# RWKV recurrences of a two-block kernel: the batches of a chunked recurrence reordered, and their triangular inverse started from blocks of 16 instead of 32

## The chip, the cores and the metric

The kernel runs on one core of a Trainium2 chip as one program. The metric is the device time of one execution in microseconds (us). Five engines work side by side, each through a list of instructions in a fixed order: PE (TensorE, matrix products), DVE (VectorE), ACT (ScalarE), POOL (GpSimd) and SP, which here only issues DMA transfers. They wait for each other through semaphores.

## What is computed

Two blocks follow each other on 512 tokens of width 1024. The first holds a Hyena branch and an RWKV-7 branch, whose gated sum goes through an output projection, and then a mixture of 16 experts. The second holds sparse attention, two feed-forward layers and an S5 layer. The change lies in the RWKV branch, and the gates that stand beside it come from the same projection:

```python
def rwkv_scan(decay, k, v, a_vec, b_vec, r, state0, reverse):
    def step(S, inp):
        w_t, k_t, v_t, a_t, b_t = inp[:5]
        sa = jnp.einsum('bhij,bhj->bhi', S, a_t)
        S = S * w_t[:, :, None, :] + sa[..., None] * b_t[:, :, None, :] + v_t[..., None] * k_t[:, :, None, :]
        y = jnp.einsum('bhij,bhj->bhi', S, inp[5]) if emit else None
        return S, y
...
def token_mixer(h, p, states0):
    cols = h @ p['w_in']
    hy_cols, rw_cols, gate_cols = jnp.split(cols, (HY_COLS, HY_COLS + RW_COLS), axis=-1)
    y_hy = hyena_branch(hy_cols, p) @ p['hy_proj']
    y_rw, finals = rwkv_branch(rw_cols, p, states0)
    g_hy, g_rw = jnp.split(jax.nn.sigmoid(gate_cols), 2, axis=-1)
    mixed = (g_hy * y_hy + g_rw * (y_rw @ p['rw_proj'])) @ p['w_out']
```

The recurrence runs over 8 heads of 64, in both directions, over 512 tokens, after a run over 256 context tokens that leaves the first states.

## The kernel before

The recurrence is cut into chunks of 64 tokens. Within a chunk the effect of the removal vectors on each other is a unit lower triangular 64x64 system; its inverse turns the chunk into a map of the state, and only those maps are applied one after the other. The work is done in six batches (`rwkv`, L627): two of the context tokens (256 columns, no read-out) and four of the latent tokens (512 columns, one group of two heads and both directions each). A batch holds 16 chunk systems and goes through these steps:

- `rw_start` (L749): projections of the hidden state (`win_mm`, PE at L614 for the context and, split in three fp32r products, at L285 to L287 for the latent tokens), neighbour mixing on DVE (L621, L622), norms through `head_rstd` (PE L726, DVE, a power on POOL at L733, PE L735 and L741), decays (PE L800, a scan on DVE L805), and the scaled vectors AR and BK.
- `rw_gram` (L845): the products of these vectors within a chunk (PE L866), masked into the tile GA (DVE L875). GA has one buffer.
- `rw_inverse` (L887): a transposition into 32x32 blocks (DVE L894), then 31 steps of substitution on DVE, each one product (L902) and one sum (L903) on 31 to 256 elements per partition.
- `rw_blocks` (L906): two transpositions (DVE L913 into X, L914 into TTt), then the lower left 32x32 block of each 64x64 inverse from 32 small products (PE L923), a copy (ACT L926), and 32 more (PE L931).
- `rw_rows` and `rw_ops` (L936, L1006): transpositions and products that build the chunk maps (PE L956 to L1023, L1036), the sum into MT (DVE L1027) and the start of SP (L1039).
- `rw_chain` (L1047): for the latent batches seven steps in each of two directions, in each a PE product (L1066) and a DVE sum (L1071), then the read-out on PE (L1084, L1087).
- `rw_end` (L701): the normalisation of the read-out (PE L707, `head_rstd` again on the tile rny, DVE L712).

The small products L923 and L931 use 32x32 quadrants of the PE array (`tile_position`), many others 64x64 quarters or all of it.

Two more pieces of PE work stand in this stage. `hy_out` (L543) projects the Hyena output. `fill` (L548) computes the gates: 16 groups of columns, each 24 fp32r products (384 in all) into the one PSUM buffer "sm", an activation on ACT into the tile hyo (one buffer), a scaling on POOL and a transfer to memory:

```python
        for w_, dst in (("wgh", self.mhd), ("wgr", self.grd)):
            for c in range(KD):
                ps = self.psum("sm", 1)
                self.h_mm(ps, I[w_][c], "wf", self.nwf, nc.gpsimd)
                g = self.rw["wk"].tile([P, T], F32, name="hyo")
                nc.scalar.activation(g, ps, AF.Tanh, scale=0.5)
```

`fill` is written last, but the program is put in order by a scheduler when it is built: it sets one order of instructions for each engine, after dependences, its own estimates and the order of writing, and puts products of `fill` and of the next batch between others. Buffers are handed out by tags with a number of buffers each; a new tile waits for the last reader of the tile whose buffer it takes. After the stage `mix_out` reads the gates back (tile mhg), projects the recurrence's output (PE L1295, L1303, tiles rwp), multiplies by the gates and goes into the output projection (PE L285 to L287 with woh, wol).

Of the kernel before, what the change touches and what calls it, by code (L numbers as in the profile page):

```python
# [12 lines left out]
F32 = mybir.dt.float32  # L13
# [4 lines left out]
AF = mybir.ActivationFunctionType  # L18
OP = mybir.AluOpType
# [47 lines left out]
def _consts():  # L67
# [31 lines left out]
    misc["gmask"] = np.where(i[None, :] < 64, s[:, None] < q, s[:, None] <= q) * 1.0  # L99
    misc["inv"] = np.repeat((10000.0 ** (-np.arange(32, dtype=f8) / 32))[None, :], P, 0)  # L100
    misc["eye16"] = (i[:, None] % 16 == np.arange(16)[None, :]) * 1.0
    misc["iota"] = np.repeat(np.arange(T)[None, :], P, 0) * 1.0
# [76 lines left out]
class K:  # L179
# [444 lines left out]
    mtag = "ch"  # L624
    nmm, nwi, nwf, wit = 2, None, 6, "w"

    def rwkv(self):  # L627
# [4 lines left out]
        es = ExitStack()  # L632
        self.nwi, self.wit = 5, "wi"
        with es:
# [26 lines left out]
            self.rw_gram(B[0])  # L661
            for i in range(len(B) + 1):
                if i < len(B):
                    self.rw_inverse(B[i])
                if i:
                    self.rw_chain(B[i - 1])
                if i and B[i - 1]["out"]:
                    self.rw_end(B[i - 1])
                if i < len(B):
                    self.rw_blocks(B[i])  # L670
                    self.rw_rows(B[i])
                if i + 1 < len(B):
                    self.rw_start(B[i + 1])
                    self.rw_gram(B[i + 1])
                if i == 0:
                    self.hy_out()
                    self.rw_gate()
# [71 lines left out]
    def rw_start(self, b):  # L749
# [23 lines left out]
        if out:  # L773
            b["kms"] = wk.tile([P, T], F32, name="kms", bufs=3)
            b["y"] = wk.tile([P, T], F32, name="yr")
# [69 lines left out]
    def rw_gram(self, b):  # L845
# [3 lines left out]
        nc, out = self.nc, b["out"]  # L849
        g = b["GA"] = self.rw["wk"].tile([P, 2, 2, 8, CH], F32, name="GA", bufs=1)  # L850
        gs = [g]
# [35 lines left out]
    def rw_inverse(self, b):  # L887
        nc, page = self.nc, self.rw_page
        V, G = nc.vector, nc.gpsimd
        GA = b["GA"]  # L890


        L = page("L", "i0").rearrange("p (t s) -> p t s", s=32)
        V.transpose(L, ap(GA, 0, [[1, 32], [32, 2], [CH, 16]]))  # L894
        Xi = page("Xi", "i1").rearrange("p (t s) -> p t s", s=32)
        G.memset(Xi, 0.0)
        G.memset(ap(Xi, 0, [[33, 32]]), 1.0)
        tmp = page("Xt", "i2", 256)
        for s in range(31):
            m, k = 31 - s, s + 1  # L900
            o = tmp[:, :m * k].rearrange("p (t s) -> p t s", s=k)
            V.tensor_tensor(o, L[:, s + 1:, s:s + 1].to_broadcast([P, m, k]), Xi[:, s:s + 1, :k].to_broadcast([P, m, k]), op=OP.mult)  # L902
            V.tensor_tensor(Xi[:, s + 1:, :k], Xi[:, s + 1:, :k], o, op=OP.add)  # L903
        b["Xi"] = Xi

    def rw_blocks(self, b):  # L906
# [3 lines left out]

        TTt = b["TTt"] = wk.tile([P, 16, 64], F32, name="TTt", bufs=1)
        X1 = page("X1", "i0").rearrange("p (u s) -> p u s", s=32)
# [4 lines left out]

        FT = page("FT", "i1", T).rearrange("p (u t) -> p u t", t=32)
        pf = self.psum("ch", 2)
# [16 lines left out]
    def rw_rows(self, b):  # L936
# [13 lines left out]
        for z, gg in enumerate(groups):  # L950
# [13 lines left out]

            AG = self.rw_page("AG", f"i{z}").rearrange("p (n h x c) -> p n h x c", n=4, h=2, x=2)
            ps = self.psum("ch", 2)
# [39 lines left out]
    def rw_ops(self, b, TA):  # L1006
# [4 lines left out]
        BKt, UV, PC, out = (b[x] for x in ("BKt", "UV", "PC", "out"))  # L1011
        MT = b["MT"] = C["wk"].tile([P, 2, 8, CH], F32, name="MT", bufs=1)
        SP = b["SP"] = C["wk"].tile([P, 16, CH], F32, name="SP", bufs=1)
# [1426 lines left out]
```

## Time and profile before

| | |
|---|---|
| median of three runs | 3376.53 us (3373.27 to 3382.11) |
| the profiled execution | 3368.45 us, span of its instructions 3366.7 us |
| PE busy | 3116.9 us, 93% |
| DVE busy | 1637.9 us, 49% |
| ACT, POOL busy | 941.6 us (28%), 733.7 us (22%) |
| mean granted PE clock | 0.95 of full speed |
| the six batches and the end of `fill` | 308 to 922 us of the span |

Busy time is the time in which an engine has an instruction under way; a wait for a semaphore isn't counted. The granted clock is the speed that the chip gave PE, as a share of its full clock. The profiled execution is 8.1 us shorter than the median of the runs, so times worked out from its rows are of its scale. The stage of the change is a fifth of the span.

### The profile page before, as it was taken

To read this page: it belongs to the slowest core of one execution; us is meant where nothing else is said; L and a number is where in the kernel's file an instruction comes from. 1 tells how busy PE (TensorE), PEld (TensorE's weight loads), DVE (VectorE), ACT (ScalarE), POOL (GpSimd) and SP (SyncE) were. 2 spreads that over 40 slices of the span, in tenths; PEclk is the share of its full clock that TensorE was granted. 3 is DMA by queue.
4 is the path that set the end of the run, shared out by engine and by line. 5 is a ranking of instruction groups with operands and counts; after the bars stand their busy time and mean duration, and the time that the engine had idled before them with its cause. 6 is when DMAs were issued, how large, how long until landed. Compare 5 with 4: busy or idle time off the path is not lost.

```text
span 3366.7 us, 42701 instructions
## 1 busy us (share of the span) xinstructions
PE 3116.9 (93%) x16973; PEld 1971.9 (59%) x16973; DVE 1637.9 (49%) x2862; ACT 941.6 (28%) x1707; POOL 733.7 (22%) x793
## 2 busy tenths in 40 slices
PE   8988989889899999999999988899898998999999
PEld 3746666656574334333333256566677777778887
DVE  3665566765361210110110156875676776456464
ACT  3313444323231111111101032245331332234242
POOL 1022233443120233330000033200695002110000
PEclk9999888888889999999999999889998998999999
DMA  5643111111469999999999954310336456322221
GB/s 218 231 168 119 57 41 58 51 35 43 150 245 382 369 421 421 421 421 421 420 421 420 421 220 152 123 57 26 116 124 232 156 194 173 122 88 91 97 100 69
DMA packets 144591, 681.41 MB, mean 202 GB/s; under 512 B 25455, under 2 KB 33815, under 8 KB 76424
## 3 DMA queue, kind: packets, MB, share of 16 engines
q1 hardware_dynamic: 134480, 652.44, 50.6%
q0 software_dynamic: 5536, 18.16, 1.5%
q10 hardware_dynamic: 4376, 8.09, 0.7%
q8 instruction: 134, 2.20, 0.3%
q14 instruction: 65, 0.53, 0.0%
HBM read 654.50 MB, written 24.12 MB: 202 GB/s over the span
## 4 chain that ended last, share of the span: by engine, by line
PE 45%; DMA 15%; DVE 7%; POOL 7%; issue 2%; ACT 2%; SPq 0%; POOLq 0%; ACTq 0%; DVEq 0%
DMA we<-in_w_dram 13%; PE mm L1638 9%; PE mm L285 4%; PE mm L286 4%; PE mm L287 4%; PE ch L1670 3%; POOL cug L2054 3%; PE tr L1552 2%; POOL sca L2055 2%; PE sm L286 1%; PE sm L287 1%; PE sm L285 1%; DMA wa<-in_adaw_dram 1%; PE sm L1601 1%; POOL qss L1896 1%
## 5 line engine op out<-in xcount | busy, mean ns | idle before, releaser
L1638 PE MATMUL mm<-we,XG 128*64 128x512 f32 x2048 | 473.6, 601 | 4.0 <-DMA we<-in_w_dram 3.2
L285 PE MATMUL mm<-hh,wh 128*128 128x512 f32 x704 | 282.6, 402 | 21.4 <-DVE vg L2008 17.0
L1638 PEld LDWEIGHTS mm<-we,XG 128*64 128x64 f32 x2048 | 134.0, 137 | 273.3 <-issue 254.3
L286 PE MATMUL mm<-hl,wh 128*128 128x512 f32 x704 | 278.3, 395 | 0.0
L1670 PE MATMUL ch<-we,hid 128*64 128x512 f32 x1024 | 263.1, 598 | 12.9 <-DMA we<-in_w_dram 12.8
L287 PE MATMUL mm<-hh,wl 128*128 128x512 f32 x704 | 272.9, 396 | 0.0
L1593 DVE SCALAR_TENSOR_TENSOR hth<-hth,tr 128x256 f32<-128x256 f32 x64 | 26.9, 421 | 394.9 <-ACT hth L1592 394.4
L1670 PEld LDWEIGHTS ch<-we,hid 128*64 128x64 f32 x1024 | 94.4, 136 | 170.5 <-issue 133.9
L285 PEld LDWEIGHTS mm<-hh,wh 128*128 128x128 f32 x704 | 134.4, 191 | 63.9 <-issue 27.6
L347 DVE SCALAR_TENSOR_TENSOR macc<-wa,cvs,macc 128x512 f32<-128x512 f32 (+1 forms) x119 | 152.6, 1298 | 20.1 <-DMA wa<-in_adaw_dram 18.2
L470 POOL TENSOR_TENSOR X<-X,gy 128x512 f32<-128x512 f32 x20 | 28.2, 1432 | 590.6 <-DVE gy L1740 590.6
L280 DVE TENSOR_TENSOR wl<-wu,wh 128x1024 fp32r<-128x1024 f32 x88 | 115.2, 1310 | 76.4 <-ACT wh L279 76.2
L287 PEld LDWEIGHTS mm<-hh,wl 128*128 128x128 f32 x704 | 134.7, 191 | 29.7
L286 PEld LDWEIGHTS mm<-hl,wh 128*128 128x128 f32 x704 | 135.2, 192 | 26.9 <-POOL hl L464 0.3
L1606 DVE TENSOR_TENSOR acc<-acc,sm 128x512 f32<-128x512 f32 x48 | 32.9, 686 | 236.4 <-PE sm L1601 236.4
L1649 ACT ACTIVATE hs<-mm 128x512 f32<-128x512 f32 x64 | 38.2, 597 | 387.0 <-PE mm L1638 387.0
L279 ACT ACTIVATE wh<-wu 128x1024 fp32r<-128x1024 f32 x88 | 93.3, 1060 | 130.6 <-PE mm L286 97.6
L287 PE MATMUL mm<-hTh,wl 128*128 128x512 f32 x208 | 89.6, 431 | 13.9 <-DVE wl L280 13.8
L280 DVE TENSOR_TENSOR wl<-wd,wh 128x1024 fp32r<-128x1024 f32 (+1 forms) x48 | 56.0, 1168 | 95.3 <-ACT wh L279 90.9
L1723 POOL TENSOR_TENSOR ess<-ess,mhalf 128x1 f32<-128x1 f32 x4 | 3.2, 791 | 442.8 <-DVE ess L1722 442.7
L279 ACT ACTIVATE wh<-wd 128x1024 fp32r<-128x1024 f32 (+1 forms) x48 | 47.5, 989 | 164.0 <-PE sm L287 75.0
L285 PE MATMUL mm<-hTh,wh 128*128 128x512 f32 x208 | 89.7, 431 | 2.6 <-ACT wh L279 1.9
(835 smaller groups left out, 6685.4 us busy)
## 6 DMA issues: line engine op xcount, KB each, us to landing
we<-in_w_dram SPq DMA_DIRECT2D x384, 1024.0 KB, 14.7
wu<-in_wupf_dram SPq DMA_DIRECT2D x44, 1024.0 KB, 4.8
wa<-in_adaw_dram SPq DMA_DIRECT2D x24, 1024.0 KB, 5.1
wa<-in_adaw_dram SPq DMA_DIRECT2D x96, 256.0 KB, 4.5
wa<-in_modw_dram SPq DMA_DIRECT2D x16, 1024.0 KB, 6.1
wd<-in_wdn_dram SPq DMA_DIRECT2D x16, 1024.0 KB, 4.7
aw<-in_awin_dram SPq DMA_DIRECT2D x12, 1024.0 KB, 5.6
wi<-in_win_dram SPq DMA_DIRECT2D x46, 256.0 KB, 2.7
```

The costliest lines, as they stand in the source:

```text
L279: self.nc.scalar.activation(h, x, AF.Copy)
L280: (E or self.nc.vector).tensor_tensor(l, x, h.bitcast(F32), op=OP.subtract)
L285: mm(ps, a[0], b[0], start=start, stop=False)
L286: mm(ps, a[0], b[1], start=False, stop=False)
L287: mm(ps, a[1], b[0], start=False, stop=stop)
L347: V.scalar_tensor_tensor(a, w, c, a, op0=OP.mult, op1=OP.add)
L1552: nc.tensor.matmul(ps[:, c * i:c * i + c], self.xn[:, t, o:o + P], oh[:, t], start=(t == 0), stop=(t == TT - 1), skip_group_check=True)
L1638: mm = nc.tensor.matmul(ps[64 * h:64 * h + 64], XG[:, k, CAP * e:CAP * e + CAP], w[:, i, h], start=(k == 0), stop=(k == KD - 1), skip_grou ...
L1649: nc.scalar.activation(hs, ps, AF.Copy)
L1670: mm = nc.tensor.matmul(py[n][64 * h:64 * h + 64], hid[h][:, f], ww[h][:, i, 512 * n:512 * n + 512], start=(f == 0), stop=(f == 15), skip_ ...
L2054: E.tensor_tensor(u[k], p[k][1], p[k][0], op=OP.mult)
L2055: E.tensor_tensor(o, u[0], u[1], op=op)
```

## The change

Six things change together. The loop over the batches is written in another order: the start and the Gram products of batch i+1 come before the inverse, blocks, rows, chain and end of batch i, where before the inverse of a batch came first, then the chain of the batch before it. GA gets two buffers. The substitution runs on the 16x16 diagonal blocks alone, both of a 32x32 block in one instruction: 15 steps of two instructions. `rw_blocks` puts the 32x32 inverses together from them: 64 products of 32x32 (after: L924), a copy on ACT, 64 products of 16 columns (L931, L934), 32 more (L939) and four masked sums on DVE (L944, L946, two of L949), ahead of the two sets of 32 products that put the 64x64 inverses together as before. Buffers are moved: wf (weights of `fill`) 6 to 4, wi 5 to 4, kms 3 to 2; TTt and MT share one buffer, FT, F and AG another. What is computed is the same.

```diff
@@ -98,6 +98,7 @@
+    misc["rm"] = np.stack([i % 64 < 16, i % 64 // 16 == 2, i % 64 // 16 == 1], 1) * 1.0
@@ -622,7 +623,7 @@
-    nmm, nwi, nwf, wit = 2, None, 6, "w"
+    nmm, nwi, nwf, wit = 2, None, 4, "w"
@@ -630,7 +631,7 @@
-        self.nwi, self.wit = 5, "wi"
+        self.nwi, self.wit = 4, "wi"
@@ -659,19 +660,16 @@
             self.rw_start(B[0])
             self.rw_gram(B[0])
-            for i in range(len(B) + 1):
-                if i < len(B):
-                    self.rw_inverse(B[i])
-                if i:
-                    self.rw_chain(B[i - 1])
-                if i and B[i - 1]["out"]:
-                    self.rw_end(B[i - 1])
-                if i < len(B):
-                    self.rw_blocks(B[i])
-                    self.rw_rows(B[i])
+            for i, b in enumerate(B):
                 if i + 1 < len(B):
                     self.rw_start(B[i + 1])
                     self.rw_gram(B[i + 1])
+                self.rw_inverse(b)
+                self.rw_blocks(b)
+                self.rw_rows(b)
+                self.rw_chain(b)
+                if b["out"]:
+                    self.rw_end(b)
@@ -771,7 +769,7 @@
-            b["kms"] = wk.tile([P, T], F32, name="kms", bufs=3)
+            b["kms"] = wk.tile([P, T], F32, name="kms", bufs=2)
@@ -847,7 +845,7 @@
-        g = b["GA"] = self.rw["wk"].tile([P, 2, 2, 8, CH], F32, name="GA", bufs=1)
+        g = b["GA"] = self.rw["wk"].tile([P, 2, 2, 8, CH], F32, name="GA", bufs=2)
@@ -896,11 +894,13 @@
-        for s in range(31):
-            m, k = 31 - s, s + 1
-            o = tmp[:, :m * k].rearrange("p (t s) -> p t s", s=k)
-            V.tensor_tensor(o, L[:, s + 1:, s:s + 1].to_broadcast([P, m, k]), Xi[:, s:s + 1, :k].to_broadcast([P, m, k]), op=OP.mult)
-            V.tensor_tensor(Xi[:, s + 1:, :k], Xi[:, s + 1:, :k], o, op=OP.add)
+        for s in range(15):
+            m, k = 15 - s, s + 1
+            o = tmp[:, :2 * m * k].rearrange("p (x t s) -> p x t s", x=2, s=k)
+            at = 32 * (s + 1)
+            V.tensor_tensor(o, ap(L, at + s, [[528, 2], [32, m], [0, k]]), ap(Xi, at - 32, [[528, 2], [0, m], [1, k]]), op=OP.mult)
+            x = ap(Xi, at, [[528, 2], [32, m], [1, k]])
+            V.tensor_tensor(x, x, o, op=OP.add)
         b["Xi"] = Xi
@@ -908,14 +908,48 @@
-        TTt = b["TTt"] = wk.tile([P, 16, 64], F32, name="TTt", bufs=1)
+        TTt = b["TTt"] = wk.tile([P, 16, 64], F32, name="TTt", tag="TM", bufs=1)
...
+        F = page("F", "ag")[:, :T].rearrange("p (u t) -> p u t", t=32)
+        quads = [(q, slice(32 * q, 32 * q + 32), 32 * (q % 2)) for q in range(4)]
+        pf = self.psum("ch", 2)
+        for u in range(16):
+            for q, qs, o in quads:
+                nc.tensor.matmul(pf[qs, 32 * u:32 * u + 32], GA[qs, 0, u // 8, u % 8, o:o + 32], X1[qs, o // 2 + u], start=True, stop=True,
+                                 skip_group_check=True, tile_position=(32 * q, 32 * q))
+        nc.scalar.activation(F, pf.rearrange("p (u t) -> p u t", t=32), AF.Copy)
+        px, pt = self.psum("ch", 2), self.psum("ch", 2)
+        for u in range(16):
+            for q, qs, o in quads:
+                if q % 2 == 0:
+                    nc.tensor.matmul(px[qs, 16 * u:16 * u + 16], TTt[qs, u, o:o + 32], F[qs, u, 0:16], start=True, stop=True,
+                                     skip_group_check=True, tile_position=(32 * q, 32 * q))
+                else:
+                    nc.tensor.matmul(px[qs, 16 * u:16 * u + 16], F[qs, u], TTt[qs, u, o + 16:o + 32], start=True, stop=True,
+                                     skip_group_check=True, tile_position=(32 * q, 32 * q))
+        for u in range(16):
+            for q, qs, o in quads:
+                if q % 2 == 0:
+                    nc.tensor.matmul(pt[qs, 16 * u:16 * u + 16], F[qs, u], TTt[qs, u, o + 16:o + 32], start=True, stop=True,
+                                     skip_group_check=True, tile_position=(32 * q, 32 * q))
+        rm = self.m("rm")
+        px = px[:, :256].rearrange("p (u t) -> p u t", t=16)
+        x = X1[:, 0:16, 0:16]
+        V.scalar_tensor_tensor(x, px, rm[:, 2:3], x, op0=OP.mult, op1=OP.add)
+        x = TTt[:, :, 48:64]
+        V.scalar_tensor_tensor(x, px, rm[:, 1:2], x, op0=OP.mult, op1=OP.add)
+        for q in (0, 2):
+            x = TTt[32 * q:32 * q + 32, :, 16:32]
+            V.scalar_tensor_tensor(x, pt[32 * q:32 * q + 32, :256].rearrange("p (u t) -> p u t", t=16), rm[32 * q:32 * q + 32, 0:1], x,
+                                   op0=OP.mult, op1=OP.add)
+
-        FT = page("FT", "i1", T).rearrange("p (u t) -> p u t", t=32)
+        FT = page("FT", "ag")[:, :T].rearrange("p (u t) -> p u t", t=32)
@@ -962,7 +996,7 @@
-            AG = self.rw_page("AG", f"i{z}").rearrange("p (n h x c) -> p n h x c", n=4, h=2, x=2)
+            AG = self.rw_page("AG", "ag").rearrange("p (n h x c) -> p n h x c", n=4, h=2, x=2)
@@ -1009,7 +1043,7 @@
-        MT = b["MT"] = C["wk"].tile([P, 2, 8, CH], F32, name="MT", bufs=1)
+        MT = b["MT"] = C["wk"].tile([P, 2, 8, CH], F32, name="MT", tag="TM", bufs=1)
```

A line L of the kernel before stands in the changed one at L-2 (between the loop and `rw_blocks`; at L+1 ahead of the loop) or, behind the new products, at L+34: the sum into MT is L1061, the chain's product L1100, its sum L1105, the projections L1329 and L1337. In the rows below, an entry "x8" is eight like instructions in a row.

The first place is DVE ahead of the sum into MT of the third batch (the first of 512 columns). Before, its rows were the neighbour mixing and the decays of the batch behind it:

```order
L622 SCALAR_TENSOR_TENSOR zv<-mm,cols,zv 128x511
L805 SCALAR_TENSOR_TENSOR th<-misc,th 128x512
L809 TENSOR_TENSOR E<-th 128x8x64
L810 TENSOR_SCALAR E<-th 128x8
L820 SCALAR_TENSOR_TENSOR ta<-ta,kk 128x512
L1027 TENSOR_TENSOR MT<-ch,misc 128x512 x2
L1039 TENSOR_TENSOR SP<-tr,PC 128x448 x2
```

In the changed kernel the same place holds the last steps of the substitution of the batch behind it (L901, L903) and its first transposition (L913):

```order
L903 TENSOR_TENSOR Xi<-Xi,Xt 128x2x3x13
L901 TENSOR_TENSOR Xt<-L,Xi 128x56
L903 TENSOR_TENSOR Xi<-Xi,Xt 128x2x2x14
L901 TENSOR_TENSOR Xt<-L,Xi 128x30
L903 TENSOR_TENSOR Xi<-Xi,Xt 128x2x15
L913 STREAM_TRANSPOSE X_4592<-Xi 128x32x32
L1061 TENSOR_TENSOR MT<-ch,misc 128x512 x2
L1073 TENSOR_TENSOR SP<-tr,PC 128x448 x2
```

The substitution has moved from beside the chain of the batch before it to ahead of that chain, during the rows of that batch.

The second place is PE in the chain of that third batch. Before, products of `fill` (those into sm) stand between the steps of the chain (L1066):

```order
L286 MATMUL sm<-hTl,wh 128x512
L287 MATMUL sm<-hTh,wl 128x512
L285 MATMUL sm<-hTh,wh 128x512
L1066 MATMUL ch<-SP,MT 64x64 x2
L286 MATMUL sm<-hTl,wh 128x512
L287 MATMUL sm<-hTh,wl 128x512
L285 MATMUL sm<-hTh,wh 128x512
L1066 MATMUL ch<-SP,MT 64x64 x2
```

In the changed kernel the first steps of the chain (L1100) have the new small products of the batch behind it between them, and the later ones projections (into mm) of the batch after that:

```order
L1100 MATMUL ch<-SP,MT 64x64 x2
L924 MATMUL ch<-X_4592,GA 32x32 x26
L1100 MATMUL ch<-SP,MT 64x64 x2
L924 MATMUL ch<-X_4592,GA 32x32 x27
L1100 MATMUL ch<-SP,MT 64x64 x2
L924 MATMUL ch<-X_4592,GA 32x32 x8
...
L288 MATMUL mm<-hTh,wl 128x512
L1100 MATMUL ch<-SP,MT 64x64 x2
L286 MATMUL mm<-hTh,wh 128x512
L287 MATMUL mm<-hTl,wh 128x512
L288 MATMUL mm<-hTh,wl 128x512
L1100 MATMUL ch<-SP,MT 64x64 x2
```

The work between the steps of a chain is now of other batches, no longer `fill`; before the last sum into MT the changed kernel has issued 86 products of `fill`, where before it were all 384.

The third place is PE at the end of the stage. Before, the last product of `fill` stands ahead of the blocks of the last batch, and the first products of `mix_out` (L1295) are put into that batch:

```order
L285 MATMUL sm<-hTh,wh 128x512
L286 MATMUL sm<-hTl,wh 128x512
L287 MATMUL sm<-hTh,wl 128x512
L1411 MATMUL sm<-rtw,mlat 128x16 x8
L923 MATMUL ch<-X_5583,GA 32x32 x32
...
L973 MATMUL ch<-misc,BK 128x128 x4
L1295 MATMUL mm<-xn_6755,rwp 128x512
L973 MATMUL ch<-misc,BK 128x128 x4
```

In the changed kernel 261 products of `fill` stand behind the last read-out (L1121), and all 24 of L1329 behind the last of these:

```order
L1121 MATMUL pp<-GR,UV 64x64 x2
L286 MATMUL sm<-hTh,wh 128x512
L287 MATMUL sm<-hTl,wh 128x512
L288 MATMUL sm<-hTh,wl 128x512
...
L287 MATMUL sm<-hTl,wh 128x512
L288 MATMUL sm<-hTh,wl 128x512
L1445 MATMUL sm<-rtw,mlat 128x16 x8
L1329 MATMUL sm<-xn_7577,rwp 128x512 x3
L1329 MATMUL tr<-xn_7577,rwp 128x512 x6
```

So the end of the stage is moved from the last batch's own end to the end of `fill` and of the projection behind it.

## Rows read from the trace of the kernel before

**Rows 1.** Windows, first batch to output projection, cut at the sums into MT

```profile
core 0: us, PE busy (x) PEld busy (x) DVE busy (x) ACT busy (x) POOL busy (x), PEclk, DMA share, GB/s
308.00:377.00 69.00, 60.99 (x509) 37.19 (x509) 44.43 (x95) 32.67 (x70) 19.39 (x24) 0.95 0.18 58
377.00:480.00 103.00, 94.14 (x744) 69.37 (x746) 66.26 (x129) 42.99 (x82) 28.39 (x28) 0.83 0.17 55
480.00:583.00 103.00, 92.85 (x752) 66.84 (x750) 70.08 (x137) 42.41 (x84) 39.60 (x35) 0.85 0.16 52
583.00:680.00 97.00, 87.22 (x920) 64.92 (x911) 65.46 (x122) 35.73 (x76) 37.24 (x38) 0.91 0.14 45
680.00:786.00 106.00, 92.70 (x914) 66.20 (x914) 62.85 (x123) 37.01 (x77) 41.88 (x41) 0.82 0.12 41
786.00:869.00 83.00, 75.80 (x875) 56.45 (x873) 48.70 (x107) 25.25 (x55) 22.40 (x26) 0.88 0.29 103
869.00:922.00 53.00, 48.92 (x394) 25.45 (x391) 16.78 (x37) 3.60 (x6) 4.45 (x5) 0.94 0.28 97
308.00:922.00 614.00, 552.62 (x5074) 386.43 (x5073) 374.56 (x748) 219.65 (x445) 193.35 (x194) 0.87 0.18 61
```

**Rows 2.** Waits of PE, 308 to 922 us: total us, times, longest us

```profile
PE mm L287 <- DVE wl L280: 10.9, 4, 4.5
PE pp L735 <- POOL rny L733: 10.6, 4, 5.2
PE sm L285 <- ACT hyo L556: 6.9, 8, 1.7
PE mm L735 <- POOL rnk L733: 6.2, 4, 2.3
PE ch L923 <- DVE X L913: 5.5, 4, 2.3
PE ch L973 <- ACT AG L969: 3.4, 5, 0.9
```

**Rows 3.** DVE in the first substitution: start us, length us, line, tiles, elements

```profile
309.83 1.95 DVE L894 STREAM_TRANSPOSE L<-GA 128x1024 f32<-128x1024 f32 x1 [0.17 <-POOL GA L880]
311.82 0.21 DVE L902 TENSOR_TENSOR Xt<-L,Xi 128x31 f32<-128x31 f32 x1
312.06 0.21 DVE L903 TENSOR_TENSOR Xi<-Xi,Xt 128x31 f32<-128x31 f32 x1
...
314.65 0.30 DVE L902 TENSOR_TENSOR Xt<-L,Xi 128x135 f32<-128x135 f32 x1
314.99 0.30 DVE L903 TENSOR_TENSOR Xi<-Xi,Xt 128x135 f32<-128x135 f32 x1
```

**Rows 4.** DVE busy on Xi's instructions (substitution, L913, L914), all six batches

```profile
310.00:920.00 610.00, 190.19 (x384) 5.58 (x10) 0.87 0.18 60
```

**Rows 5.** PE timeline, blocks of the fifth batch

```profile
763.80 1.20 PE L923 MATMUL ch<-X,GA 32*32 32x32 f32 x64 [2.35 <-DVE X L913]
764.93 0.50 PE L286 MATMUL sm<-hTl,wh 128*128 128x512 f32 x1
765.26 0.40 PE L287 MATMUL sm<-hTh,wl 128*128 128x512 f32 x1
765.50 0.57 PE L285 MATMUL sm<-hTh,wh 128*128 128x512 f32 x1
765.87 0.63 PE L286 MATMUL sm<-hTl,wh 128*128 128x512 f32 x1
766.29 0.63 PE L287 MATMUL sm<-hTh,wl 128*128 128x512 f32 x1
766.85 1.96 PE L931 MATMUL ch<-TTt,FT 32*32 32x32 f32 x64
768.75 0.69 PE L956 MATMUL ch<-misc,zv 128*128 128x128 f32 x2
```

**Rows 6.** PE timeline, fill between two of its groups

```profile
754.87 0.39 PE L285 MATMUL sm<-hTh,wh 128*128 128x512 f32 x1
755.10 0.39 PE L286 MATMUL sm<-hTl,wh 128*128 128x512 f32 x1
755.32 0.39 PE L287 MATMUL sm<-hTh,wl 128*128 128x512 f32 x1
756.84 0.50 PE L285 MATMUL sm<-hTh,wh 128*128 128x512 f32 x1 [1.13 <-ACT hyo L556]
```

**Rows 7.** PE timeline, products behind quarter-array products

```profile
690.14 0.33 PE L1066 MATMUL ch<-SP,MT 64*64 64x64 f32 x4
690.40 0.50 PE L286 MATMUL mm<-hTl,wh 128*128 128x512 f32 x1
690.74 0.40 PE L287 MATMUL mm<-hTh,wl 128*128 128x512 f32 x1
```

**Rows 8.** PE timeline, end of the stage and first output products

```profile
919.00 1.88 PE L1303 MATMUL ch<-xn,rwp 128*128 128x512 f32 x4
920.72 1.88 PE L1303 MATMUL mm<-xn,rwp 128*128 128x512 f32 x4
922.04 0.80 PE L285 MATMUL sm<-woh,mTh 128*128 128x512 f32 x1
...
926.08 0.80 PE L285 MATMUL ch<-woh,mTh 128*128 128x512 f32 x1 [2.32 <-DVE mhg L1307]
```

## The prediction

> **What bounds the kernel now.** I read the windows first, cut where the sums into MT start, because each batch has one and the change moves everything between them. From 308 to 922 us the stage takes 614 us; PE is busy for 552.6 of them at a mean granted clock of 0.87, DVE for 374.6 [rows 1]. So 61.4 us are waits of PE, and of the busy time 0.13 x 552.6 = 72 us are lost to the lower clock; what is left, 481 us, is work at full speed. PE is therefore the bound, but a loose one: 133 of 614 us are not work. The chip's clock and the waits hang together as far as the rows show it: the blocks of the fifth batch begin behind a wait of 2.35 us for X, and the products after it go from 0.23 us each to 0.43 (765.87 to 766.29), the second of the two clock levels (1.2 instead of 2.4 GHz) [rows 5]. Next I read who is waited for. The largest are DVE's wl, 10.9 us, and X, 5.5 us; POOL's powers rny and rnk, 10.6 and 6.2; ACT's hyo, 6.9 [rows 2]. The first two come from DVE being filled with the substitution while the chain of the batch before runs beside it.
>
> Behind the stage nothing else changes, and the rest of the program starts from its end, so I take every microsecond of 922 as one of the total.
>
> **DVE's part of the change.** All instructions on Xi take 190.2 us [rows 4]. Six times L913 and L914 are in that, which work on as many elements as L894 at 1.95 us [rows 3]: 23.4 us. The substitution is thus 166.8 us, 27.8 a batch. The new one has 30 instructions of 30 to 128 elements; rows of 31 and 135 elements last 0.21 and 0.30 and start 0.24 and 0.34 apart [rows 3], so 0.28 each, 8.4 a batch, and four masked sums of 256 elements, at about 0.5 each by the same rows carried further, 2 us. DVE gets 17 us a batch back. It is no gain by itself, since DVE is busy for 61% of the stage; it counts where PE waits for DVE, and in when the chain can start.
>
> **PE's part.** 160 products are added per batch. Thirty-two of L923 (two passes each, so the row shows 64) take 1.13 us, from 763.80 to the start of the next instruction [rows 5]. Five such sets in six batches are 30 x 1.13 = 34 us. The rows bound this from both sides: 30 x 1.9 = 57 us, if they run at the lower clock as L931 did there (766.85 to 768.75) [rows 5]; and, since the new ones go to up to four quadrants where the old ones went to two, and 96 have half the columns, half of 34, 17 us. I take 34, because the columns differ more than the instruction does in these rows.
>
> **The order.** This is the larger part. I counted the products between the sums into MT in the two orders and priced each kind by its full-clock start-to-start time (0.228 for a product of fill [rows 6], 0.43 for a pass of L1303 and so 0.86 for the product [rows 8], 0.035 for a quadrant product). Before, the five intervals hold 75.5, 74.1, 76.5, 74.9 and 63.0 us, together 364; they took from 377 to 869, 492 us [rows 1]. So 128 us are lost, 25.6 an interval. In the new order they hold 76.5, 57.9, 70.9, 68.8 and 51.5, together 325.6, although 28 us of new products are in that, because most of fill has left them.
>
> What will an interval lose? From 25.6 I take off the waits for wl and X, 16.4 / 5 = 3.3; the hyo waits that leave with fill, 6.9 / 5 = 1.4; and part of the clock. The clock cost in the whole stage is 72 us, 3 of them in the first window (0.05 x 61) [rows 1] and 3 in the last (0.06 x 49), so 13 an interval. With fewer waits I take 7.5, half way between 13 and 0.05 x 65 = 3, rounded down. That leaves 25.6 - 3.3 - 1.4 - 5.5 = 15.4. The new steps put back some: L957 is queued behind two masked sums, and those behind L931's products and an ACT copy; the nearest wait, for AG from ACT, is 3.4 / 5 = 0.7 us each [rows 2], so I add 0.6. POOL's powers stay, 16.8 us in all: the scheduler has put other work behind them, but PE's order is fixed and what follows them waits too. Sixteen us per interval: 325.6 + 80 = 406 instead of 492, **86 us less**.
>
> The chain supports that order of size. The substitution now stands ahead of MT, where DVE must finish it before the chain may start, and this is the wait that the change adds. From the last Gram product to MT the new order has about 13 us of PE work; DVE has 8.4 + 1.95 + 1.95 = 12.3 us. They are level, so I charge nothing; if DVE is late, the chain and the whole next interval are late with it.
>
> **The first sum into MT.** The substitution of the first batch is 19 us shorter, but the start of the second batch stands ahead of its corrections, and PE has the Hyena products to do anyway (61 of 69 us busy) [rows 1]. I take 3 us less; bounds are 0 and 9.
>
> **The end.** What left the batches comes back here. Before, from the last MT to the end of the stage 53 us pass (869 to 922) [rows 1]. In the new order the last chain, its read-out and 298 products of fill are 87 us (68 of them fill), then 32 products of L1329 and L1337 at 0.86, 27.5. Fill has one hyo: at each of 11 changes of group PE waits 1.13 us [rows 6], 12.4 us. Another 4 us stand, as an estimate, for the last norm's power (10.6 / 4 = 2.6 [rows 2]) and eight short products of L1445. Together 131 us, **78 more** than before. Here the cover is gone: before, those products cost nothing while PE would have waited.
>
> **Behind the end**, four of the gates' tiles are loaded during fill, so the 2.32 us for mhg and about 0.8 for wol [rows 8] can go: 3 less.
>
> **Sum.** -3 - 86 + 78 - 3 = **-14 us**. From the profiled 3368.45 this is 3354.5; the median of the runs lies 8.1 higher, so 3362. The point from which the sign turns is a loss of 18.8 us an interval instead of 16.
>
> **A rule that speaks against it.** Behind a group of quarter-array products the first full product starts its successor after 0.34 us instead of 0.23 [rows 7, 6]: 0.11 more. The new order changes between 32x32 quadrants and other sizes 142 times, the old one 30 times; 112 x 0.11 = 12 us. (The Trainium skill, "TensorEngine Tiling (Array Packing)", Key Properties, says that a change of tiling mode drains TensorE; the trace agrees for the one pair of modes in rows 7. By it the sum would be -2 us.) Part of these changes replace ones between 64x64 groups and full products that the old order had, so I give it only as a part of the second rival.
>
> **The rivals.**
>
> *Padding lost (slower).* The place is the five intervals. Fill stood in the gaps between chain steps and behind the powers; without it these become waits, and each wait of 2 us is followed by a stretch at the lower clock [rows 5]. If the loss stays at 25.6 an interval, the sum is -14 + 5 x 9.6 = +34 us, 3410; at 21 it is +11. For it: 261 of 384 fill products now come last, and the powers' 16.8 us stay. Against it: between the chain's steps stand three projections of 0.23 us each, about as much as a step allows, so the gaps are not empty.
>
> *The new products eat it (no change).* At the lower clock they cost 57 instead of 34, and the changes of size 12: -14 + 23 = +9 or, with half of each, about 0: 3372 to 3386. For it: L931 was at half clock in this very place [rows 5]. Against: many of them are now put between projections, one dense stretch of work.
>
> *Denser than I take it (much faster).* If PE waits only for the powers (16.8 / 5 = 3.4) and the clock costs 5, with 1 for the rest, the loss is about 9.5 an interval: -14 - 32 = -46 us, 3330. For it: DVE gets 17 us a batch back, and nothing on PE waits for wl in the chain. Against: no interval between two sums granted over 0.91, and the lowest has 0.82 [rows 1].
>
> *The end runs worse.* If fill's groups are fed late (weights split on POOL and DVE, four buffers instead of six), each group takes 8 us instead of 5.5 + 1.1: +15 us, no change in all.
>
> **Chances and range.** About the sum 0.36, denser 0.17, new products or end 0.24, padding lost 0.23. Under 0.3% (10 us) a measurement here can't tell from no change. A spread of some 10 us about -14 leaves part of the first case within it. Faster 0.53, same 0.22, slower 0.25. The likeliest case alone is 3350 to 3374. The range has to reach the denser case and the near half of the padding case: 3318 to 3396.
>
> **What would show it.** In the changed kernel: the five intervals between the sums into MT near 81 us each (before 98), and PE's waits for wl and X there under 5 us together; the first MT near 374, the last one near 780; from there to the first product with woh about 131 us, with waits for hyo near 1.1 us; a new set of 32 quadrant products near 1.13 us. Wrong would be: intervals over 84; a granted clock under 0.85 in them; PE waiting for MT because DVE still has the substitution; or groups of fill over 7 us apart at the end.

## The result and the profile after

The changed kernel is slower: the ratio of its runs to those of before is 1.0095, interval 1.0077 to 1.0114; the medians of five runs each are 3413.1 (3399.33 to 3415.01) and 3374.53 us. Below, a ratio's distance from 1 is given in us as its share of 3375 us: this one is 32 us. The forecast was 14 us less, with a range up to 3396; the time lies outside it, near the 3410 us of the rival of lost padding.

Windows of the changed kernel, cut as in [rows 1]: the five intervals between the sums into MT, then larger pieces (columns as there):

```profile
380.50:475.30 94.80, 88.99 (x1087) 61.27 (x1085) 54.13 (x103) 41.58 (x84) 23.01 (x24) 0.93 0.15 49
475.30:543.20 67.90, 64.47 (x958) 46.91 (x959) 49.40 (x99) 33.80 (x70) 17.27 (x16) 0.92 0.08 25
543.20:631.20 88.00, 82.34 (x1201) 59.60 (x1197) 52.23 (x106) 35.78 (x73) 24.54 (x21) 0.88 0.08 26
631.20:730.10 98.90, 91.64 (x1180) 66.64 (x1180) 56.21 (x104) 34.93 (x72) 27.19 (x26) 0.76 0.07 23
730.10:789.90 59.80, 56.09 (x1005) 41.57 (x1007) 13.75 (x32) 19.49 (x41) 17.12 (x20) 0.89 0.13 42
...
308.00:380.50 72.50, 68.51 (x901) 48.76 (x902) 50.12 (x110) 35.80 (x74) 18.70 (x24) 0.81 0.16 52
380.50:790.00 409.50, 383.63 (x5428) 276.08 (x5428) 225.81 (x440) 165.68 (x340) 109.12 (x107) 0.87 0.10 33
790.00:951.00 161.00, 134.22 (x714) 83.89 (x710) 19.07 (x40) 26.15 (x42) 59.35 (x64) 0.93 0.44 157
308.00:951.00 643.00, 586.36 (x7029) 408.73 (x7028) 295.00 (x588) 227.63 (x455) 187.18 (x195) 0.88 0.19 66
```

The intervals take 409.5 us; forecast were 406, before 492. The stage nevertheless ends at 951 instead of 922, since the end takes 161 us instead of 53, where 131 were forecast. DVE is busy for 295 us in the stage (before 374.6), PE for 586 (552.6): PE's waits are 56.6 us (61.4), and 0.12 x 586 = 70 us go to the clock (72). PE's work at full speed thus grew by 35 us, 516 instead of 481, and waits and clock together shrank by only 7: that makes the 29 us of the stage. The profiled spans differ by 44 us (those of the runs, by the ratio, by 32); the other 15 lie behind the stage. From the first output product to the end of the span the profiled runs of these kernels need 2445 (before) to 2464 us, also some of those that end the stage early. Some 8 of the 15 stand in the first 100 us: PE runs at half clock from 1008 to 1043 us, before from 984 to 1001, and half of the 17 us more is lost. Why, no run shows; the other 7 are open too.

Waits of PE from the last sum into MT to the output projection:

```profile
PE sm L288 <- POOL wl L281: 9.1, 11, 1.6
PE sm L1329 <- DVE xn L1320: 7.8, 1, 7.8
PE sm L286 <- ACT hyo L557: 7.3, 11, 0.7
PE pp L733 <- POOL rny L731: 1.4, 1, 1.4
```

PE's timeline there, in the middle of a group of fill and at its end, with SP's between them:

```profile
860.07 0.40 PE L287 MATMUL sm<-hTl,wh 128*128 128x512 f32 x1
861.23 0.50 PE L288 MATMUL sm<-hTh,wl 128*128 128x512 f32 x1 [0.76 <-POOL wl L281]
...
910.01 0.40 PE L288 MATMUL sm<-hTh,wl 128*128 128x512 f32 x1
911.15 2.00 PE L1445 MATMUL sm<-rtw,mlat 128*128 128x16 f32 x16 [0.74 <-ACT hyo L557]
920.92 4.60 PE L1329 MATMUL sm<-xn,rwp 128*128 128x512 f32 x5 [7.77 <-DVE xn L1320]
```

```profile
910.44 0.33 SPq L1316 DMA_DIRECT2D xn<-rgd  x1
910.81 1.60 SPq L1319 DMA_DIRECT2D xn<-yrd  x3
```

A late group of fill takes some 7.75 us for 24 x 0.228 = 5.5 us of work: it waits in its middle for wl (its weights, two split parts and the next load share four buffers) and at its end for hyo. And the load of xn starts 0.2 us behind the last product of fill: in the program's order it waits for PE, because xn takes the memory of the hidden state hT that fill reads. Before, that load stood at 843.84 us, also 0.2 us behind fill's last product (843.42 + 0.23), but under the last batch.

### The profile page after: what moved, and what is told of

It reads as the page before. It is cut to its first block, busy times and chain, and to the rows that moved or that the text cites. A ratio compares the mean times of both kernels' runs of the same rounds, so it can differ in the third digit from the quotient of the medians.

```text
span 3411.1 us, 46407 instructions
## 1 busy us (share of the span) xinstructions
PE 3164.6 (93%) x18893; PEld 2001.4 (59%) x18893; DVE 1555.9 (46%) x2694; ACT 947.5 (28%) x1713; POOL 725.4 (21%) x793
## 4 chain that ended last, share of the span: by engine, by line
PE 63%; DMA 16%; DVE 12%; POOL 3%; ACT 3%; issue 3%; SPq 0%; ACTq 0%; POOLq 0%; DVEq 0%
DMA we<-in_w_dram 13%; PE mm L1672 9%; PE mm L286 7%; PE mm L287 6%; PE mm L288 6%; PE ch L1704 3%; PE sm L288 2%; PE sm L287 2%; PE sm L286 2%; PE tr L1586 2%; DMA wa<-in_adaw_dram 1%; DVE macc L348 1%; PE tr L864 1%; DMA wa<-in_modw_dram 1%; DVE wl L281 1%
```

## The experiments

Every kernel is put in order anew when it is built, so that an edit also moves other instructions; that is a limit to each comparison.

**First: order, blocks, and where fill stands.** Four kernels tell apart three theories: the end costs (1), the new products cost (2), the order costs (3).

```diff
-            self.fill(None)
+                self.fill(*[(0, 3), (3, 6), (6, 9), (9, 12), (12, 16), (0, 0)][i])   # in the loop over i
```

> The changed kernel with the 16 groups of fill written after the batches (3, 3, 3, 3, 4) instead of last; the order then has all 384 products of fill ahead of the last sum into MT, and the products of L1329 inside the last batch. Theory 1 (the end costs: fill's groups run 7.75 us apart there instead of 5.47, the loads behind them come 7.8 us late, and nothing covers the last batch): about 35 us less than the changed kernel, near 3378 us. Theory 2 (the new small products and their effect on the clock cost the time wherever fill stands): within 10 us of the changed kernel, about 3410 us.

Measured: 1.0159 (1.0122 to 1.0196), 22 us slower than the changed kernel. The end fell to 62 us, 9.6 of them a wait for the output projection's weights (woh), but the five intervals grew from 409.5 to 539 us, by 129 us for 298 products of 0.228 = 68 us. My theory 1 fell: fill isn't cheaper between the new batches.

```diff
-        for s in range(15):    (and F to the four masked sums)
+        for s in range(31):    (the substitution of before)
```

> The changed kernel with the 31-step substitution of blocks of 32 back and the 160 new products, their copy and four sums taken out. Theory 1: 34 us of products go, but DVE needs 27.8 instead of 8.4 us ahead of each MT, and most of fill stays at the end (173 products behind the last read-out): 3385 to 3400 us. Theory 2: all of the loss is in the new products, so near 3370 us. Theory 3 (the order itself costs, by the substitution ahead of MT): 3410 us or more.

Measured: 1.0028 (1.0011 to 1.0045), +9 us, by its median (3389.24) in theory 1's range. The order with its buffers thus costs 9 us here.

```diff
-            for i, b in enumerate(B): ...
+            for i in range(len(B) + 1): ...    (loop, pages and buffer numbers of before)
```

> The kernel before, with its loop and its buffers, and the substitution on blocks of 16 with the new products. Its order leaves 227 products of fill behind the last read-out. Theory 1: the end costs as in the changed kernel, with the six wf buffers of before a little less, and 34 us of products are added: 3395 to 3410 us. Theory 2: 34 to 46 us over before: 3408 to 3420 us. Theory 3: near 3375 us, since the old order has no substitution ahead of MT.

Measured: 1.0066 (1.0046 to 1.0087), +22 us. So 9 and 22 make up the 32: two thirds come with the blocks. The 9 hold the order and the smaller buffers together; a kernel in the new order with the buffers of before was not run.

Both of the first two edits together (blocks of 32, fill after the batches):

> The new order with blocks of 32 and fill written after the batches: both suspected costs away. Theory 1: 34 + 35 us less than the changed kernel and some wait of MT for DVE back: 3345 to 3360 us, under the kernel before. Theory 2: near 3370. Theory 3: over 3390, as the order alone costs.

Measured: 1.0058 (1.0035 to 1.0080), 10 us over the same kernel with late fill; PE waited 10 us for woh, whose load stood behind those of the gates. With that load written ahead:

```diff
+                wos.append(mt.tile([P, 2048], F32, name="wo", bufs=2))
+                nc.sync.dma_start(wos[-1], I["wo"][:, k0:k0 + 2].rearrange("p k c -> p (k c)"))   # ahead of the loop over c
```

> The new order with blocks of 32 and fill written after the batches, and the first two loads of wo written ahead of those of the gates, where the same kernel without that waited 10 us for woh at the start of the output projection. The wait goes: 10 us less than that kernel, near 3383 us; with that it is still no faster than the kernel before by any theory, unless its batches are shorter than its one look showed.

Measured: 1.0048 (1.0028 to 1.0067), 3 us less, within the intervals: a miss, though the wait for woh is gone.

**Second: what the products cost.**

```diff
-        F = page("F", "ag") ...    (F, 160 products, four masked sums)
```

> The changed kernel without the 160 new products of each batch, their copy and the four masked sums: the inverse keeps its 16x16 diagonal blocks alone, so the part of the computation that joins them is left out. It prices the new products with the short substitution and the new order kept. Theory 1 (the new products are 34 us of work on the engine that bounds the stage, and their low-clock part comes on top): 34 to 45 us under the changed kernel, 3368 to 3380 us. Theory 2 (they cost half or less, being small; the order is what costs): 15 us or less, 3395 us or more.

Measured: 1.0069 (1.0043 to 1.0096), only 9 us less than the changed kernel, as theory 2 had it; the two intervals overlap. Its stage shows where the products went: work at full speed falls by 25 us (516 to 491), but PE's waits rise by 6 (57 to 63) and what the clock takes by 17 (70 to 87). The same edit in the old order, with its loop and buffers:

> The order and the buffers of before with the substitution of 16x16 blocks alone and no new products; as in the run without corrections, the part that joins the blocks is left out. It shows what DVE's 17 us a batch are worth where PE's work is the same as before. Theory 1 (PE bounds the stage): at most the 16 us of PE's waits for wl and X, 3358 to 3374 us. If DVE were the bound after all: 60 us or more under before, 3315 us or less.

Measured: 0.9913 (0.9886 to 0.9939), 29 us under before, between the two figures expected. With the old order the corrections thus cost 22.3 + 29.4 = 52 us, with the new 9; the two don't add up to one price.

```diff
-        for u in range(16):
+        for u in [u for u in range(16) for _ in range(2)]:    (three loops)
```

> The changed kernel with each of the 160 new products of a batch issued twice into the same place; nothing else is changed. Theory 1: another 34 us or more, 3445 to 3460 us. Theory 2: 17 us or less, since the products go into gaps and to other quadrants: under 3430 us.

Measured: 1.0298 (1.0270 to 1.0326), 69 us over the changed kernel.

```diff
+        pf, px = self.psum("ch", 2), self.psum("ch", 2)    (160 products into these, result unused)
         FT = page("FT", "i1", T).rearrange("p (u t) -> p u t", t=32)
```

> The kernel before, as it was, with 160 products like the new ones added to each batch (64 of 32 columns, 96 of 16) that go into two PSUM tiles of their own; three DVE copies of four elements read them and nothing uses the result. The substitution, the order and fill stay. It prices the products as PE's work, without the chain of copy and masked sums behind them. Theory 1 (they are work on the bound engine, with the clock part on top): 34 to 57 us over before, 3409 to 3432 us. Theory 2 (they fit into gaps and only the new chain of steps costs): under 15 us, below 3390 us.

Measured: 1.0167 (1.0138 to 1.0195), 56 us, the upper end. Three of the four comparisons thus give 52 to 69 us for 160 products a batch, one and a half to two times the 34 of the forecast, and one gives 9. The products themselves don't take that long: in the changed kernel's trace PE is busy for 14.3 us with those of L924 and for 21.1 us with all that use F, 35 us at both clock levels together. The rest is around them: in the stage of the kernel before with the products added PE's waits rise by 10 us and the clock's part by 17, with the products doubled by 5 and by 53.

**Third: is fill padding?**

```diff
-    nmm, nwi, nwf, wit = 2, None, 6, "w"
+    nmm, nwi, nwf, wit = 2, None, 4, "w"    (and wi 5 to 4, kms 3 to 2)
```

> The kernel before with the buffer numbers of the changed one (wf 4, wi 4, kms 2) and nothing else. The looks at the end of the changed kernel show 0.77 us of waiting for wl in each half group of fill with four wf buffers, none with six. If the buffers are a part of the order's cost, 5 to 12 us over before, 3380 to 3387 us; if fill is hidden in the batches here, no change.

Measured: 1.0054 (1.0033 to 1.0075), 18 us, more than expected and more than half of the 32; PE's waits for fill's wl rise to 15.4 us where the waits in the view of [rows 2] had none of this kind. What the same buffers cost in the changed kernel, no run shows apart.

```diff
-                self.h_mm(ps, I[w_][c], "wf", self.nwf, nc.gpsimd)
+                self.thin_mm(ps, I[w_][c], nc.gpsimd)    # 3 of 24 products
```

> The kernel before with fill cut to 3 of its 24 products a group (48 instead of 384 in all, 77 us of products at full clock left out, so the gates are wrong on that account); everything behind it stays. If fill is padding that costs nothing in the batches (the rival of lost padding): 30 us or less under before, 3345 us or more. If PE bounds the batches throughout: 77 us or more under before, below 3300 us.

Measured: 1.0024 (1.0011 to 1.0037): with 77 us of products taken out it is 8 us *slower*. Waits of PE in its stage, and windows of its intervals:

```profile
PE ch L1074 <- DVE SP L1079: 24.6, 33, 5.5
PE mm L1303 <- DVE xn L1294: 19.8, 2, 9.9
PE mm L287 <- DVE wl L280: 14.2, 4, 6.9
PE ch L931 <- DVE X L921: 11.5, 5, 5.1
```

```profile
382.00:877.00 495.00, 376.53 (x3848) 274.88 (x3847) 311.25 (x617) 173.57 (x354) 151.03 (x150) 0.74 0.14 48
```

PE's busy time falls from 443 (the sum of the intervals in [rows 1]) to 377 us, and the intervals stay at 495 (492): PE now waits for the chain's sums SP and for X from DVE, and the granted clock falls from 0.86 to 0.74. In the intervals its waits rise by 69 us (from 49 to 118), and what the clock costs, half of the time in which PE is busy at half clock, rises from 64 to 86. So the row doesn't show whether the chain alone would hold 492 us at full clock. The 19.8 us for xn are a projection that the new build puts too early, which none of the other kernels with the cut does; without them fill's cut would have saved some 12 us (an estimate, 19.8 - 8), far from 77.

The same edit in the changed kernel:

> The changed kernel with fill cut in the same way (3 of 24 products a group, the rest of the gates left out). Its batches hold few products of fill, and 261 of 384 stand at the end, 7.75 us a group. Lost padding: 90 to 105 us under the changed kernel, 3308 to 3323 us, so it would then be under the kernel before with the same cut. PE bound throughout: 77 to 95 us less, and the distance to the cut kernel before stays at 30 to 40 us.

Measured: 0.9883 (0.9859 to 0.9907), 72 us less than the changed kernel, below both forecasts, and 48 us under the cut kernel before (some 28 without that kernel's waits for xn), a change of sign. Its row of the intervals:

```profile
379.00:808.00 429.00, 392.69 (x5371) 280.05 (x5368) 236.83 (x439) 175.26 (x358) 144.49 (x148) 0.81 0.14 45
```

They aren't shorter for it but 20 us longer than the 409.5 with fill, at a clock of 0.81 instead of 0.87; the end, 65 us instead of 161, gives back 96. By these two rows fill costs nothing within the batches here either; at the end, where nothing covers it, it costs more than its work. The same edit in the two kernels with one half of the change shows which half gives the shorter batches:

> The old order with the new blocks and fill cut to 3 of 24 products a group (the rest of the gates left out). Theory P (padding: before is bound by its chain of dependences, and the short substitution is what shortens the batches): near the changed kernel with the same cut, 3330 to 3350 us. Theory O (the order shortens them): near the kernel before with the same cut, 3370 to 3390 us.

> The new order with blocks of 32 and fill cut in the same way. Theory P: little shorter than the kernel before with the cut, 3360 to 3385 us. Theory O: 3320 to 3345 us, as the order alone gives the shorter batches.

Measured: 0.9837 (0.9795 to 0.9879) and 0.9879 (0.9834 to 0.9924). Both halves do, each about as well as both together; so theory P was right about the blocks, theory O about the order:

| | with fill | fill cut | cost of fill's 77 us |
|---|---|---|---|
| before | 1.0000 | 1.0024 | -8 us |
| new order, old blocks | 1.0028 | 0.9879 | 50 us |
| old order, new blocks | 1.0066 | 0.9837 | 77 us |
| both (the changed kernel) | 1.0095 | 0.9883 | 72 us |

**Fourth: can the shorter batches be kept?**

The old order with the new blocks, and fill written after the batches as in the first edit:

> The old order and its six buffers with the new blocks, and fill written after the batches (3, 3, 3, 3, 4 groups), so that all 384 products stand ahead of the last sum into MT. If fill can be padding in these shorter batches too, the end falls from 141 to some 55 us and the batches grow by less: 3340 to 3370 us, faster than before. If the shorter batches have no room left, 3395 us or more, as the same move in the new order was 18 us slower.

Measured: 1.0256 (1.0209 to 1.0303), the worst place for fill: 64 us more than with late fill. The windows of the intervals, of that kernel and then of the one with late fill:

```profile
363.00:947.00 584.00, 533.26 (x5808) 383.21 (x5808) 259.10 (x477) 189.12 (x381) 169.59 (x172) 0.78 0.15 52
```

```profile
367.00:803.00 436.00, 411.01 (x5549) 294.25 (x5551) 231.53 (x475) 171.95 (x351) 120.05 (x121) 0.85 0.10 34
```

The intervals grow by 148 us: the full-speed work in them by 0.78 x 533 - 0.85 x 411 = 66, the waits by 26, the clock's share by the rest, 56.

```diff
-    nmm, nwi, nwf, wit = 2, None, 6, "w"
+    nmm, nwi, nwf, wit = 2, None, 8, "w"    (the kernel before, TTt and MT in one buffer)
```

> The kernel before with one buffer for TTt and MT, as the change has it, and the memory given to wf: 8 buffers instead of 6. If what less buffers cost goes on upward, 5 to 15 us under before; if six are enough, within 5 us of before.

Measured: 1.0011 (0.9990 to 1.0033), no change: six buffers are enough.

```diff
-                ps = self.psum("sm", 1)
+                late = (dst is self.grd or c > 4) and c % 2
+                ps = self.psum("mm", self.nmm) if late else self.psum("sm", 1)
```

> The changed kernel with every other late group of fill in a PSUM tile of the ring mm, so that PE doesn't wait for ACT to empty sm. If the feeding of the groups is the end's 30 us: the waits for hyo at the end, 7.3 us, and a part of the pauses at wl go, 8 to 14 us less, 3399 to 3405 us. If PE then waits for wl instead, since four wf buffers hold one half group, less than 5 us.

> The old order with the new blocks, one buffer for TTt and MT, two of hyo, and the second PSUM tile for every other late group. Waits for hyo, 11.8 us, go: near 3390 us. The wait for xn behind the last product of fill, 7.9 us, stays, so it is not expected to come under the kernel before.

Measured: 1.0074 (1.0053 to 1.0095) and 1.0042 (1.0019 to 1.0065), 7 and 8 us less than without, though the intervals overlap. In the first PE's waits for hyo at the end fall from 7.3 to 0.4 us, but others take their place:

```profile
PE sm L1330 <- DVE xn L1321: 10.5, 1, 10.5
PE mm L288 <- POOL wl L281: 7.1, 9, 1.6
PE sm L288 <- POOL wl L281: 6.6, 10, 0.9
```

Those for wl are now 13.7 us (9.1), those for xn 10.5 (7.8). The end is 158.6 us long (161.0) in the first and 140.0 (141.1 without the edit) in the second, so most of the 7 and 8 us didn't come from the end, and these runs don't show that the feeding of the groups sets its length. No version found that computes the same is under the kernel before.

## Why the prediction failed

**The sum, term by term.** On the scale of the profiled executions 14 us less were forecast and 44 more came, 58 off. Of these the first sum into MT has 6.5, the intervals 3.5, the end 30 and what lies behind it 18. So the step that failed is the end: 131 us were charged for fill, the last chain and the projection, and they took 161, with waits for wl and xn and a lower clock that the sum put at nothing. The second is "I take every microsecond of 922 as one of the total": 15 us came up behind the stage, 8 of them at the lower clock.

**What bounds the kernel.** "PE is therefore the bound, but a loose one" didn't hold for the kernel before. Busy for 90% of its stage, PE was filled with products that the batches left room for: taking 77 us of them out gains nothing by the runs, some 12 us without the waits for xn. That DVE's substitution has a part in the pace is shown: with the short one, no joining products and the old order 29 us go, and with fill cut the new blocks are 63 us faster than the old ones in the old order (43 without the waits for xn); in the new order they are equal. That the chain through DVE (substitution, X, SP) alone sets the 492 us is argued, not shown, since with fill cut PE also loses more to the lower clock. The forecast moved fill's 68 us from the batches to the end at the same price; the batches had had it for next to nothing, and the end paid more than its work.

**The intervals.** 406 forecast, 409.5 measured: work 325.6 and a loss of 16.8 us each where 16 stood. DVE's substitution ahead of MT, priced at nothing, cost PE at most 3.5 us (its waits for the sums into MT). That the sum fits is in part luck: the clock's part was put too low (0.13 x 384 = 50 us instead of 37), the waits too high (42 instead of 26). Half way between 13 and 3 is 8, not 7.5; that is 2.5 us in the sum. DVE got back the forecast 17 us a batch (190.2 us on Xi before, 71.7 and 11.4 for the masked sums now).

**The new products.** Taken at 34 us, and PE is busy with them for 35, partly at the lower clock. What they cost the kernel is 52 to 69 us in three comparisons, through waits and the clock around them, and 9 in one, where work taken out came back as such. The half-clock rival was thus right that the lower clock adds to them; its two additions, 23 and 12 us, together make +21 us, not the +9 that it gives. That changes of tile size cost 12 us was not shown by any run apart, and 0.34 us isn't peculiar to them: it also stands behind a mere wait (861.23 us above, where the next product starts at 861.57).

**The first sum into MT** was 3.5 us later (380.5) instead of 3 earlier: PE's waits in the window are 4 us instead of 8, but the clock takes 13 us at 0.81 instead of 3 at 0.95. The new products stand in it.

**The end** is the term that was mis-sized: 131 forecast, 161 measured. It has 27 us of waits, 8 for the clock (PE is busy at half clock for 15 us there) and 126 of work at full speed; the sum had 15, nothing and some 116. The waits for wl are 9.1 and for xn 7.8, both put at nothing; those for hyo, 7.3, were under the 12.4 charged. The lower clock stands at 820 to 840 us (0.74) and behind the wait for xn, where the first six passes of the projection are 0.87 us apart instead of 0.43. Of the ten us more work the first product after each of 22 pauses, 0.34 instead of 0.23 us, is 2; the others aren't assigned. The old order with the new blocks has six wf buffers and no wait for wl at its end, which speaks for the four buffers as the cause of those. I had named slow feeding as a rival at 15 us, near what came of it, but not that the load of xn can't start before fill's last product.

**Behind the end**, the 3 us didn't come: PE waits 3.9 us for wol (before 1.3, which [rows 8] don't show) and 1.4 for mhg (2.3). The 8 us at the lower clock behind that had no term.

**The rival of lost padding** had the right name and sign, but its place was wrong: the intervals didn't keep their loss of 25.6 us. That its figure, 3410, fits is luck, since its 48 us were to stand there. What was lost is the free ride of fill, which costs -8 us before and 72 after, against batches that are 48 us shorter without it. 80 - 48 = 32 restates the four ratios and is no check of them, and without the waits for xn in the cut kernel before it would read some 60 - 28. Why fill costs twice its work between the shorter batches is answered only in part (clock 56, waits 26); why the order's share differs with and without corrections, and what part of the 32 the smaller buffers have (18 us on the kernel before), stays open.

## What to carry to other kernels

A high busy share doesn't make an engine the bound: ask which of its work could be taken away without the time moving, and if a piece is padding, cut it in a trial before counting on moving it. When a dependence chain is shortened, the work that hid under it must be paid somewhere; the gain is the chain's shortening less what that work costs where it then stands, and here that cost was larger. And look at what a moved step holds: memory that the next stage needs turned a free load into a wait of 7.8 us.

## What the runs showed of the chip that was not expected

The granted clock didn't follow the waits one for one. In the kernel with fill between the new batches, PE waits for 3.4 us in two pauses from 422 to 434 and stays at full clock. After a third pause of 1.6 us, up to 442.4, it runs at the half for 48 us while it is busy nearly all of the time (windows of 6 us; the clock is the third column from the end):

```profile
428.00:434.00 6.00, 4.16 (x18) 3.06 (x17) 1.07 (x1) 0.63 (x1) 5.00 (x6) 1.00 0.52 156
434.00:440.00 6.00, 6.00 (x54) 5.01 (x56) 0.91 (x3) 2.64 (x5) 3.68 (x4) 1.00 0.30 106
440.00:446.00 6.00, 4.43 (x68) 3.20 (x53) 1.66 (x4) 1.54 (x3) 2.32 (x3) 0.68 0.42 134
446.00:452.00 6.00, 6.00 (x29) 2.30 (x26) 2.86 (x4) 2.81 (x5) 0.73 (x1) 0.50 0.00 0
452.00:458.00 6.00, 6.00 (x179) 4.26 (x179) 5.54 (x8) 3.57 (x6) 2.13 (x2) 0.50 0.02 4
...
482.00:488.00 6.00, 6.00 (x41) 5.00 (x41) 2.52 (x7) 2.23 (x5) 3.92 (x4) 0.50 0.00 0
488.00:494.00 6.00, 5.92 (x68) 4.90 (x64) 5.55 (x15) 4.39 (x12) 0.90 (x2) 0.84 0.01 3
```

The same stretch in windows of 2 us around the third pause (columns: us, PE busy, PEclk, DMA share, GB/s):

```profile
440.00:442.00 2.00, 0.82 (x47) 1.00 0.87 270
442.00:444.00 2.00, 1.61 (x5) 0.53 0.34 123
```

The stage of the kernel before has sixteen shorter stretches at half clock, the longest 17 us. Fewer waits thus don't mean less time at the lower clock: the stage lost 72 us to it before with 61 us of waits, 70 after with 57, and 97 (0.16 x 608) with 58 where fill stands between the new batches. Nor do fewer products: with fill cut in the kernel before it lost 103, with 132 us of waits.
